# A hybrid encoder layer with 32 experts on one core: the token lists' entries, the buffers of gathered rows and the place of a visit's first transposes are changed

## The chip, the cores and the metric

The kernel runs on one core of a Trainium2 chip, as one launch. The metric is the device time of a launch in microseconds; smaller is better.

## What is computed

One layer over x of 1024 tokens by 1024 features, float32. First comes the mixer: a modulated norm, one projection, windowed attention with a sink and neighbourhood attention side by side, an output projection and a gated residual. Then comes a mixture of 32 experts of which each token takes four, and a final norm. The reference for the second part, cut:

```python
def moe_ffn(h, w_router, b_router, w_gate_up, b_gate_up, w_down, b_down):
    logits = (xt @ w_router + b_router).astype(jnp.float32)
    top_val, top_idx = lax.top_k(logits, TOP_K)          # 4 of 32
    gates = jax.nn.softmax(top_val, axis=-1)
    ...
    def expert_block(args):
        xb, e = args
        gu = xb @ w_gate_up[e] + b_gate_up[e]
        gate = jnp.minimum(gu[:, :D_FF], SWIGLU_LIMIT)
        up = jnp.clip(gu[:, D_FF:], -SWIGLU_LIMIT, SWIGLU_LIMIT)
        glu = gate * jax.nn.sigmoid(SWIGLU_ALPHA * gate)
        return ((up + 1.0) * glu) @ w_down[e] + b_down[e]
    ...
    y = jax.ops.segment_sum(ys * slot_gate[:, None].astype(ys.dtype), slot_tok, num_segments=t + 1)[:t]
```

## The kernel before

**Precision.** Large products are made of three: each float32 operand is split into a rounded part (`hi`) and the remainder (`lo`), and hi·hi, hi·lo and lo·hi are added up in PSUM.

**Output projection and routing.** Until about 560 us the mixer is computed. Then the eight token tiles of 128 go through a pipeline of stages, each some steps behind the one before: `mix` (first 512 columns of the output projection, through `half`), `mix_on` (the other 512, then the norm of the experts' input, stored to `d_h`), `turn_h` (transposes), `logits`, `top`, `places`, `gates_y`, `first_y`. `half` multiplies the projection by the gate and adds it to x: L1016 evicts the PSUM tile `pab`, L1017 and L1018 are the product and the sum, on POOL for the first half of a tile and on DVE for the second. `places` makes four list entries per token: `pi` (L1092) is the position in the experts' list, `pair` (L1094, L1095) holds the row number and the gate. POOL scatters them to the lists `d_l` in HBM (L1097, an indirect DMA per choice), and `first_y` uses `pair` once more as the rows of a scatter-add into `d_y` (L1126). `pi` has two buffers and `pair` has three, so a tile's entries can be written only when the DMAs of an earlier tile have read theirs.

**The first expert, early.** After four tiles `lead` picks the fullest expert so far, starts the load of its first weights (L1181), reads 256 entries of its list (L1160) and gathers their rows into two `xg` tiles (L1164). `xform` transposes them on PE (L1366) and splits them into `xH` and `xL` (L243 on ACT, L244 on DVE). Its products are put between those of the last tiles' routing.

**The visits.** `rank` sorts the experts by load, and `experts` makes a visit to each: wide visits (stream H: several row blocks, weights stationary or moving, L1532 to L1534 and L1557) and narrow ones (stream L, at most 128 rows, L236 to L238). A visit is cut into pieces, (visit, gate/up or down, column, k half), and the pieces of the two streams are merged into one list. For piece m, `load` issues the weights on SP (1 MB each, L1181 or L1184), `cook` makes their hi part on ACT (L1305) and their lo part on DVE and POOL (L1307), and `mm` issues the products. Cooking runs five pieces ahead of the products (`LOOK`). Raw and cooked weights lie in ten slots, of which the first 32 pieces use two for their loads. Before a visit, `get_lists` reads its lists (L1317, SP), `get_rows` gathers its rows into an `xg` tile (L1347, POOL), one of two buffers, and `xform` transposes them. `leave` adds the result to `d_y` (L1490, POOL). At piece 12 (`BEGUN`) the first narrow visit is prepared: lists, gather, transposes, bias. Every later visit is prepared while its stream's previous visit runs: its first gather stands one step before the last gate/up piece, then each down piece issues the next gather and the transposes of the current block.

The order of each engine's instructions is set by a scheduler that works on the order in which the code is written and on the buffers.

Of the kernel before, what the change touches and what calls it, by code (L numbers as in the profile page):

```python
# [5 lines left out]
F32 = mybir.dt.float32  # L6
F32R = mybir.dt.float32r
I32 = mybir.dt.int32
U32 = mybir.dt.uint32
AF = mybir.ActivationFunctionType  # L10
ALU = mybir.AluOpType
# [4 lines left out]
D = 1024  # L16
S = 1024
NT = 8
# [13 lines left out]
NP = 8 // KP  # L32
# [194 lines left out]
class Kernel:  # L227
# [771 lines left out]
    def half(self, x, m):  # L999
        nc, pq, bc, wo, i = self.nc, self.pq, self.bc, self.wo, x["i"]  # L1000
        V, A, P = nc.vector, nc.scalar, nc.gpsimd
        ts = slice(i * 128, (i + 1) * 128)
        cs = slice(512 * m, 512 * m + 512)
        xt, ya = x["xt"][:, cs], x["ya"][:, cs]
        pp = [self.pm.tile([128, 512], F32, name="pab", bufs=4) for _ in range(2)]
        for a in range(2):
            for k in range(4 * a, 4 * a + 4):
                last = self.mm3(pp[a], self.oh[:, k, ts], self.ol[:, k, ts], wo[k][0][:, cs], wo[k][1][:, cs],
                         k % 4 == 0, k % 4 == 3)
        if i == m == 0:  # L1010
            with self.tc.issue_after(last):
                self.sum_squares(1, self.sq, pq.tile([128, 512], F32, name="pt", bufs=1)[:, 0:2 * NT])
            A.activation(self.sqr, self.sums, AF.Sqrt, bias=self.eps, scale=1.0 / 512)
            V.reciprocal(self.sqr, self.sqr)
        A.activation(ya, pp[0], AF.Copy, scale=self.sqr[:, 0, i:i + 1])
        V.scalar_tensor_tensor(ya, pp[1], self.sqr[:, 1, i:i + 1], ya, op0=ALU.mult, op1=ALU.add)  # L1016
        (V if m else P).tensor_tensor(ya, ya, bc["gate_m"][:, cs], op=ALU.mult)  # L1017
        (V if m else P).tensor_tensor(xt, xt, ya, op=ALU.add)  # L1018
        A.activation(ya, xt, AF.Square, accum_out=x["ss"][:, m:m + 1])

    def mix_on(self, x, **_):
# [58 lines left out]
    def places(self, x, macc, gd, lo32, ie, ip, **_):  # L1080

        nc, qp, pr, w, oh, mk, i = self.nc, self.qp, x["pr"], x["w"], x["oh"], x["mk"], x["i"]
        V, P, T = nc.vector, nc.gpsimd, nc.tensor
        ixf, gt = w[:, 0, :], w[:, 1, :]
        T.matmul(pr[:, 192:224], lo32, mk, start=True, stop=False)
        T.matmul(pr[:, 192:224], self.ones, macc, start=False, stop=True)
        V.tensor_tensor(macc, macc, mk, op=ALU.add)
        rk = qp.tile([128, 4, 32], F32, name="rk", bufs=2)
        V.tensor_tensor(rk, oh, pr[:, None, 192:224].to_broadcast([128, 4, 32]), op=ALU.mult)
        V.tensor_reduce(w[:, 4, :], rk, axis=AX.X, op=ALU.add)  # L1090
        pi = qp.tile([128, 4], I32, name="pi", bufs=2)
        V.scalar_tensor_tensor(pi, ixf, float(PITCH), w[:, 4, :], op0=ALU.mult, op1=ALU.add)  # L1092
        pair = x["pair"] = qp.tile([128, 4, 2], I32, name="pair", bufs=3)
        V.tensor_scalar(pair[:, :, 0], ip.to_broadcast([128, 4]), float(PITCH + 128 * i), None, op0=ALU.add)  # L1094
        V.tensor_copy(pair.bitcast(F32)[:, :, 1], gt)  # L1095
        for j in range(4):
            s = P.indirect_dma_start(out=self.d_l, out_offset=bass.IndirectOffsetOnAxis(ap=pi[:, j:j + 1], axis=0),  # L1097
                                     in_=pair[:, j, :], in_offset=None)
            for o in self.scat:
                self.tc.declare_no_dep(s.ins, o.ins, reason="other rows of the lists")  # L1100
            self.scat.append(s)
        V.tensor_tensor(rk, oh, gt[:, :, None].to_broadcast([128, 4, 32]), op=ALU.mult)
        V.tensor_reduce(gd[:, i, :], rk.rearrange("p j e -> p e j"), axis=AX.X, op=ALU.add)
# [143 lines left out]
    def experts(self):  # L1247
# [10 lines left out]
            for x, y in zip(mine, mine[1:]):  # L1258
                nxt[x] = y
        regs, raw, cooked, lists, blk, biases, late = {}, {}, {}, {}, {}, {}, []  # L1260
        xs, hs, accs, gates = {}, {}, {}, {}
        self.pe_time = 0.0
        led = self.led
        regs[0] = led["reg"]
# [76 lines left out]
        def get_rows(n, j):  # L1341

            st, r, blocks = vis[n]
            off, nt = blocks[j]
            ls = lists[n][j]
            xg = self.ep.tile([128, D], F32, name="xg", bufs=2)
            P.indirect_dma_start(out=xg[:nt], out_offset=None, in_=self.d_h2,  # L1347
                                 in_offset=bass.IndirectOffsetOnAxis(ap=ls[:nt, 0:1], axis=0))
            blk.setdefault(n, []).append(dict(n=n, j=j, nt=nt, ls=ls, xg=xg))
# [57 lines left out]
        def xform(b):  # L1407
            n, j = b["n"], b["j"]
            if j == 0:
                xs[n] = parts("x", n)  # L1410
            turn(b["xg"][:b["nt"]], xs[n][1][j][1:], b["nt"], 0, n == 0)
# [168 lines left out]
        for m in range(-LOOK, M):  # L1580
            if m == BEGUN:
                lp = pools["lp"] = tc.alloc_tile_pool(name="lp", bufs=1, side="right", reuse_waits="tile")
                pw = tc.alloc_tile_pool(name="pw", bufs=1, space=PSUM, reuse_waits="tile")
            for j, i in loads_at.get(m, []):
                load(j, i)
            if m < 0:
                cook(m + LOOK)
                continue
            if m == BEGUN:
                n = first[1]  # L1590
                get_lists(n)
                for j in range(len(vis[n][2])):
                    get_rows(n, j)
                    xform(blk[n][j])
                get_bias(n)
                mates = no_mates()
                for b in blk[n]:
                    b["mates"] = mates
                for n in first:
                    get_lists(nxt[n])  # L1600
            n, kind, c, kh = seq[m]
            if m + LOOK < M:
                cook(m + LOOK)
            mm(m)
            if m < BEGUN:
                yield
            if n in nxt:
                q = nxt[n]
                nb = len(vis[q][2])
                at = todo.setdefault(n, 0)  # L1610
                if kind == "g" and c == 3 and kh == NP - 2:
                    if q in nxt:
                        get_lists(nxt[q])
                    get_rows(q, 0)
                if kind == "d":
                    if at < nb:
                        if at + 1 < nb:
                            get_rows(q, at + 1)
                        xform(blk[q][at])
                    if at == 0:  # L1620
                        get_bias(q)
                    if at == 2 * NP - 1:
                        mates = no_mates()
                        for b in blk[q]:
                            b["mates"] = mates
                    todo[n] = at + 1
# [115 lines left out]
```

## Time and profile before

| | |
|---|---|
| runs | 2266.4, 2270.0, 2276.2 us (median 2270.0) |
| profiled execution | 2269.7 us; span 2268.0 us, mean granted clock 0.969 |
| PE busy | 2084.2 us (92%) |
| DVE, POOL, ACT busy | 1568.2 (69%), 1111.3 (49%), 949.6 us (42%) |
| HBM | 518 MB read, 59 MB written, 254 GB/s over the span |

PE is TensorE, DVE VectorE, ACT ScalarE, POOL GpSimd and SP the engine that issues most DMAs; PEld is TensorE's weight load. Times count from the start of the span. An instruction stands as line, operation and output<-input, and the L numbers are lines of the kernel before. A granted clock of 1.00 is 2.4 GHz, 0.50 is 1.2 GHz. Busy shares are averages over stages with different limits, so the rows below are given by stage.

### The profile page before, as it was taken

What the parts mean: (1) busy time and instruction counts of PE and PEld (TensorE: products, weight loads), DVE (VectorE), ACT (ScalarE), POOL (GpSimd) and SP (SyncE); (2) the same over time, 40 slices, a digit from 0 to 9 for tenths busy, and PEclk for the clock granted to TensorE, in tenths of its full rate; (3) what the DMA queues carried; (4) which work ended last, traced back from release to release, by engine and by line L of the source; (5) the groups of instructions that cost most, each with busy time, mean ns of one, the idle gap of its engine ahead of it and who ended that gap; (6) DMA issues with size and microseconds to landing.
All of it is one profiled execution on the core that took longest, in us unless ns stands there. A gap on an engine that the chain in (4) does not pass through costs nothing. (4 is left out here: it accounts for less than half of the span.)

```text
span 2268.0 us, 34804 instructions
## 1 busy us (share of the span) xinstructions
PE 2084.2 (92%) x12090; PEld 1533.8 (68%) x12090; DVE 1568.2 (69%) x2790; ACT 949.6 (42%) x1612; POOL 1111.3 (49%) x959
## 2 busy tenths in 40 slices
PE   6999999999787998888879999999999999999973
PEld 3987777777576876665546555566686777877772
DVE  3777646876585699787866454455686868878975
ACT  3543436764353456554643121222233434345543
POOL 2522123543555567778874334333536455555453
PEclk8999999999899999999989999999999999999987
DMA  9555577823556699898879998999898898898775
GB/s 320 157 166 149 163 217 198 159 78 124 152 164 191 233 298 307 278 293 256 299 225 368 371 320 292 344 347 329 263 347 265 309 315 307 304 313 298 257 251 188
DMA packets 325114, 579.17 MB, mean 255 GB/s; under 512 B 40009, under 2 KB 78089, under 8 KB 322577
## 3 DMA queue, kind: packets, MB, share of 16 engines
q1 hardware_dynamic: 301529, 524.22, 67.7%
q0 software_dynamic: 23408, 52.71, 11.2%
q8 instruction: 97, 1.59, 0.3%
q14 instruction: 80, 0.66, 0.1%
HBM read 518.23 MB, written 58.92 MB: 254 GB/s over the span
## 5 line engine op out<-in xcount | busy, mean ns | idle before, releaser
L1307 POOL TENSOR_TENSOR w<-w,w 128x288 fp32r<-128x288 f32 x456 | 599.9, 1366 | 547.7 <-ACT w L1305 523.6
L1305 ACT ACTIVATE w<-w 128x1024 fp32r<-128x1024 f32 x456 | 469.1, 1054 | 525.3 <-DMA w<-in_w_gate_up 123.8
L1307 DVE TENSOR_TENSOR w<-w,w 128x736 fp32r<-128x736 f32 x456 | 504.8, 1119 | 214.1 <-ACT w L1305 211.9
L1534 PE MATMUL accH<-xH,w 128*128 128x256 f32 (+9 forms) x1408 | 396.8, 294 | 5.1 <-POOL w L1307 4.1
L1532 PE MATMUL accH<-xH,w 128*128 128x256 f32 (+6 forms) x1024 | 320.6, 316 | 2.2 <-ACT xH L243 0.6
L1533 PE MATMUL accH<-xH,w 128*128 128x256 f32 (+6 forms) x1024 | 315.2, 309 | 0.3 <-DVE xH L244 0.3
L1534 PEld LDWEIGHTS accH<-xH,w 128*128 128x128 f32 x1408 | 267.0, 191 | 18.3 <-POOL w L1307 4.8
L1532 PEld LDWEIGHTS accH<-xH,w 128*128 128x128 f32 x1024 | 193.0, 189 | 50.5 <-issue 27.4
L1533 PEld LDWEIGHTS accH<-xH,w 128*128 128x128 f32 x1024 | 193.7, 189 | 5.1 <-DVE xH L244 0.7
L1557 PE MATMUL accL<-w,xL 128*32 128x512 f32 (+3 forms) x896 | 176.9, 599 | 1.2 <-issue 0.8
L236 PE MATMUL accH<-w,hH 128*128 128x512 f32 (+3 forms) x368 | 150.1, 410 | 5.1 <-ACT w L1305 5.1
L237 PE MATMUL accH<-w,hH 128*128 128x512 f32 (+3 forms) x368 | 146.8, 399 | 0.0
L238 PE MATMUL accH<-w,hH 128*128 128x512 f32 (+3 forms) x368 | 143.2, 401 | 1.0 <-POOL w L1307 1.0
L238 PE MATMUL accL<-w,xL 128*72 128x512 f32 (+4 forms) x256 | 106.5, 416 | 39.9 <-POOL w L1307 28.6
L1530 PE MATMUL accH<-xH,w 128*128 128x416 f32 (+2 forms) x384 | 110.6, 365 | 10.1 <-DVE t L1422 10.0
L1490 POOL DMA_INDIRECT d_y<-y,lsH x54 | 96.6, 1789 | 45.6 <-DVE y L1484 32.9
L236 PE MATMUL accL<-w,xL 128*72 128x512 f32 (+4 forms) x256 | 104.3, 407 | 2.2 <-ACT w L1305 1.1
L1449 DVE TENSOR_TENSOR t<-accL,biasL 32x512 f32<-32x512 f32 (+8 forms) x88 | 60.5, 688 | 64.2 <-PE accL L1557 45.4
L236 PEld LDWEIGHTS accH<-w,hH 128*128 128x128 f32 (+3 forms) x368 | 68.4, 186 | 52.4 <-issue 19.2
L237 PE MATMUL accL<-w,xL 128*72 128x512 f32 (+4 forms) x256 | 103.4, 404 | 0.0
L1557 PEld LDWEIGHTS accL<-w,xL 128*32 128x32 f32 (+3 forms) x896 | 39.5, 115 | 84.6 <-issue 79.0
L237 PE MATMUL pm<-whi,hl 128*128 128x256 f32 x320 | 92.5, 290 | 1.4 <-DVE hl L244 1.2
(362 smaller groups left out, 4422.7 us busy)
## 6 DMA issues: line engine op xcount, KB each, us to landing
w<-in_w_gate_up SPq DMA_DIRECT2D x264, 1024.0 KB
w<-in_w_down SPq DMA_DIRECT2D x132, 1024.0 KB
aw<-in_w_ada SPq DMA_DIRECT2D x64, 256.0 KB
wraw<-in_w_in SPq DMA_DIRECT2D x18, 512.0 KB
xt<-in_x SPq DMA_DIRECT2D x16, 512.0 KB
wa<-in_w_ada SPq DMA_DIRECT2D x8, 1024.0 KB
d_h<-zero SPq DMA_DIRECT2D x9, 512.0 KB
d_y<-zero SPq DMA_DIRECT2D x18, 256.0 KB
```

What stands on the lines that cost most here:

```text
L236: mm(ps, lh, rh, start=start, stop=False)
L237: mm(ps, ll, rh, start=False, stop=False)
L238: return mm(ps, lh, rl, start=False, stop=stop).ins
L1305: A.activation(hi, w, AF.Copy)
L1307: eng.tensor_tensor(lo[:, :, cs], w[:, :, cs], hi[:, :, cs].bitcast(F32), op=ALU.subtract)
L1449: V.tensor_tensor(t, p[o:o + nt], bv[o:o + nt], op=ALU.add)
L1490: s = P.indirect_dma_start(out=self.d_y[c], out_offset=bass.IndirectOffsetOnAxis(ap=b["ls"][:nt, 0:1], axis=0), in_=y, in_offset=None, com ...
L1530: mm(p[:, :2 * sp], hi[:, k, ws], x[:, :, kk, :], start=kk == 0, stop=False)
L1532: mm(p[:, :sp], hi[:, k, ws], x[:, 0, kk, :], start=kk == 0, stop=False)
L1533: mm(p[:, :sp], hi[:, k, ws], x[:, 1, kk, :], start=False, stop=False)
L1534: mm(p[:, :sp], lo[:, k, ws], x[:, 0, kk, :], start=False, stop=kk == 7)
L1557: mm(p[o:o + nt], w[:, kk, :], hi[:, k, :], start=kk < len(at), stop=kk >= 8 - len(at))
```

## The change

Five edits. The products L1017 and L1018 of the last tile's first half move from POOL to DVE. `pi` and `pair` get a buffer for each of the eight tiles. Every third gather uses a tile `xg3` of its own. The first narrow visit's transposes are written three pieces after its gather. Of a later visit with several blocks the second gather is written with the last gate/up piece, and in the down pieces a block's transposes stand before the gather of the block after next.

```diff
@@ half
-        (V if m else P).tensor_tensor(ya, ya, bc["gate_m"][:, cs], op=ALU.mult)
-        (V if m else P).tensor_tensor(xt, xt, ya, op=ALU.add)
+        e = V if m or i == NT - 1 else P
+        e.tensor_tensor(ya, ya, bc["gate_m"][:, cs], op=ALU.mult)
+        e.tensor_tensor(xt, xt, ya, op=ALU.add)
@@ places
-        pi = qp.tile([128, 4], I32, name="pi", bufs=2)
+        pi = qp.tile([128, 4], I32, name="pi", bufs=NT)
...
-        pair = x["pair"] = qp.tile([128, 4, 2], I32, name="pair", bufs=3)
+        pair = x["pair"] = qp.tile([128, 4, 2], I32, name="pair", bufs=NT)
@@ experts: get_rows
-            xg = self.ep.tile([128, D], F32, name="xg", bufs=2)
+            got.append(n)
+            xg = (self.ep.tile([128, D], F32, name="xg", bufs=2) if len(got) % 3 else
+                  wp.tile([128, D], F32, name="xg3"))
@@ experts: the loop over pieces
             if m == BEGUN:
                 n = first[1]
                 get_lists(n)
-                for j in range(len(vis[n][2])):
-                    get_rows(n, j)
-                    xform(blk[n][j])
+                get_rows(n, 0)
+                blk[n][0]["mates"] = no_mates()
                 get_bias(n)
-                mates = no_mates()
-                for b in blk[n]:
-                    b["mates"] = mates
                 for n in first:
                     get_lists(nxt[n])
+            if m == BEGUN + 3:
+                xform(blk[first[1]][0])
...
+                if kind == "g" and c == 3 and kh == NP - 1 and nb > 1:
+                    get_rows(q, 1)
                 if kind == "d":
                     if at < nb:
-                        if at + 1 < nb:
-                            get_rows(q, at + 1)
                         xform(blk[q][at])
+                        if at + 2 < nb:
+                            get_rows(q, at + 2)
```

In the order rows below the changed kernel's lines are two to four higher (L1092 is L1094, L1094 is L1096, L1305 is L1307, L1347 is L1351, L1366 is L1370).

DVE, at the last tile's output projection, before. `ip` is the token number within a tile, `rk` and `gd` belong to the gates, `lg` are the next tile's logits.

```order
L1092 SCALAR_TENSOR_TENSOR pi<-w 128x4
L1102 TENSOR_TENSOR rk<-ohot,w 128x128
L1103 TENSOR_REDUCE gd<-rk 128x32
L1094 TENSOR_SCALAR pair<-ip 128x4
L1016 SCALAR_TENSOR_TENSOR ya<-pab,sqr,ya 128x512
L1062 COPY lg<-pr 128x32
```

The same place in the changed kernel:

```order
L1094 SCALAR_TENSOR_TENSOR pi<-w 128x4
L1104 TENSOR_TENSOR rk<-ohot,w 128x128
L1105 TENSOR_REDUCE gd<-rk 128x32
L1016 SCALAR_TENSOR_TENSOR ya<-pab,sqr,ya 128x512
L1064 COPY lg<-pr 128x32
L1019 TENSOR_TENSOR ya<-ya,gate_m 128x512
```

The write of the row numbers is gone from here. All eight (`L1096 TENSOR_SCALAR pair<-ip 128x4 x8`) now stand together ahead of the routing. The eviction L1016 of the last half tile follows the gates directly, and the product and sum of the first half (L1019, L1020) stand some rows earlier on DVE.

ACT, when the first narrow visit's rows have been transposed, before. `hH` is the first expert's activation, `xL<-pt` the narrow visit's split, `w_...` are pieces of weights copied:

```order
L243 ACTIVATE hH<-ga 128x256 x4
L243 ACTIVATE xL<-pt 128x512 x2
L1305 ACTIVATE w_7514<-w_7287 128x1024
L1305 ACTIVATE w_7548<-w_7408 128x1024
L1305 ACTIVATE w_7625<-w_7546 128x1024
```

And now:

```order
L243 ACTIVATE hH<-ga 128x256 x4
L1307 ACTIVATE w_7499<-w_7287 128x1024
L1307 ACTIVATE w_7533<-w_7408 128x1024
L243 ACTIVATE xL<-pt 128x512 x2
L1307 ACTIVATE w_7625<-w_7531 128x1024
```

The two splits moved behind two copies, those of the next two down pieces.

ACT a little later, up to the start of the second wide visit, before; `xH<-pt` are the splits of that visit's row blocks:

```order
L243 ACTIVATE xH<-pt 128x4x128 x2
L1305 ACTIVATE w_7778<-w_7715 128x1024
L1305 ACTIVATE w_7800<-w_7715 128x1024
L1305 ACTIVATE w_7820<-w_7776 128x1024
L1305 ACTIVATE w_7836<-w_7776 128x1024
L243 ACTIVATE xH<-pt 128x4x128
L1305 ACTIVATE w_7858<-w_7818 128x1024
L1305 ACTIVATE w_7880<-w_7818 128x1024
L243 ACTIVATE xH<-pt 128x4x128
L243 ACTIVATE xH<-pt 128x8x56
L1305 ACTIVATE w_7914<-w_7852 128x1024
```

And now:

```order
L243 ACTIVATE xH<-pt 128x4x128 x2
L1307 ACTIVATE w_7719<-w_7608 128x1024
L1307 ACTIVATE w_7749<-w_7608 128x1024
L1307 ACTIVATE w_7778<-w_7717 128x1024
L1307 ACTIVATE w_7800<-w_7717 128x1024
L243 ACTIVATE xH<-pt 128x4x128 x2
L1307 ACTIVATE w_7820<-w_7776 128x1024
L1307 ACTIVATE w_7836<-w_7776 128x1024
L243 ACTIVATE xH<-pt 128x8x56
L1307 ACTIVATE w_7858<-w_7818 128x1024
```

The third block's two splits, which stood behind w_7836 and behind w_7880, stand now together ahead of w_7820; the last block's (8x56) moved ahead of w_7858 and w_7880.

On PE the narrow visit's eight transposes (L1366, now L1370) have not moved: they stand behind the ranking's two small products and ahead of the first product of the next down piece in both. On POOL the wide visit's third gather (56 rows of lsH) moved ahead of two subtractions (L1307) and two scatter-adds (L1490), and the next narrow visit's gather (120 rows of lsL) ahead of six subtractions, a scatter-add and a clear. L1017 and L1018 of the last tile no longer stand there between the first expert's gathers and the next scatters.

## Rows read from the trace of the kernel before

**Rows 1.** Windows by stage: length; busy PE, PEld, DVE, ACT, POOL; clock; DMA share; GB/s
```profile
567.00:612.00 45.00, 39.64 (x187) 30.60 (x187) 29.32 (x84) 14.68 (x30) 22.90 (x18) 0.92 0.45 124
612.00:634.50 22.50, 9.49 (x47) 7.07 (x46) 9.73 (x23) 9.97 (x19) 11.97 (x12) 0.70 0.62 172
634.50:700.00 65.50, 59.59 (x456) 55.44 (x455) 56.97 (x137) 29.44 (x49) 42.57 (x37) 1.00 0.65 175
700.00:740.00 40.00, 26.31 (x118) 20.98 (x118) 20.41 (x35) 15.59 (x19) 21.09 (x17) 0.85 0.65 197
1190.00:2150.00 960.00, 951.38 (x5430) 651.50 (x5429) 643.35 (x1030) 319.33 (x476) 429.79 (x335) 1.00 0.92 315
```

**Rows 2.** Waits, 567 to 640 us: waiter, releaser, total us, times, longest us
```profile
DVE pair L1094 <- DMA d_l<-pair,pi: 18.3, 2, 12.7
DVE pair L1094 <- DMA d_y<-yi,pair: 7.1, 2, 3.9
```

**Rows 3.** DVE's timeline: start, length, instruction, idle time before it and releaser
```profile
567.33 0.17 DVE L1094 TENSOR_SCALAR pair<-ip 128x4 int32<-128x4 f32 x1 [3.91 <-DMA d_y<-yi,pair]
580.14 0.17 DVE L1094 TENSOR_SCALAR pair<-ip 128x4 int32<-128x4 f32 x1 [5.59 <-DMA d_l<-pair,pi]
627.20 0.17 DVE L1094 TENSOR_SCALAR pair<-ip 128x4 int32<-128x4 f32 x1 [12.68 <-DMA d_l<-pair,pi]
627.30 0.75 DVE L1016 SCALAR_TENSOR_TENSOR ya<-pab,sqr,ya 128x512 f32<-128x512 f32 x1
```

**Rows 4.** PE's timeline at the first expert's transposes and first product
```profile
615.68 2.82 PE L1366 MATMUL accH<-idt,xg 128*128 128x128 f32 x12 [0.82 <-DMA xg<-d_h,ls]
628.11 1.12 PE L1366 MATMUL accH<-idt,xg 128*128 128x128 f32 x4 [9.61 <-DVE ya L1016]
633.21 0.36 PE L1532 MATMUL accH<-xH,w 128*128 128x256 f32 x1 [0.53 <-DVE xH L244]
```

**Rows 5.** POOL's timeline: the last scatter of tile 3, the gather of its lists
```profile
600.79 1.32 POOL L1097 DMA_INDIRECT d_l<-pair,pi  x1 [0.30 <-issue]
609.56 1.76 POOL L1164 DMA_INDIRECT xg<-d_h,ls  x1 [7.44 <-DMA ls<-d_l]
```

**Rows 6.** PE's timeline at the first narrow visit
```profile
704.29 1.97 PE L1366 MATMUL pt<-idt,xg 128*128 128x128 f32 x8 [4.33 <-DMA xg<-d_h,lsL]
707.89 0.80 PE L236 MATMUL accH<-w,hH 128*128 128x512 f32 x1 [1.63 <-ACT w L1305]
...
738.21 1.07 PE L1366 MATMUL pt<-idt,xg 56*128 56x56 f32 x8 [7.14 <-issue]
739.92 1.41 PE L1532 MATMUL accH<-xH,w 128*128 128x312 f32 x4 [0.63 <-ACT xH L243]
```

**Rows 7.** Windows, the stretch at half clock around the second wide visit's start
```profile
734.70:744.90 10.20, 5.76 (x24) 5.23 (x25) 6.47 (x9) 4.82 (x7) 9.03 (x8) 0.50 0.57 171
```

**Rows 8.** ACT's timeline: copies of the weight pieces that come late
```profile
714.61 2.01 ACT L1305 ACTIVATE w<-w 128x1024 fp32r<-128x1024 f32 x2 [5.83 <-DMA w<-in_w_down]
721.95 2.01 ACT L1305 ACTIVATE w<-w 128x1024 fp32r<-128x1024 f32 x2 [5.33 <-DMA w<-in_w_down]
734.00 2.00 ACT L1305 ACTIVATE w<-w 128x1024 fp32r<-128x1024 f32 x2 [6.89 <-DMA w<-in_w_gate_up]
735.91 0.58 ACT L243 ACTIVATE xH<-pt 128x512 fp32r<-128x512 f32 x1
```

**Rows 9.** SP's timeline: when the loads of two of them went out
```profile
709.48 0.41 SPq L1184 DMA_DIRECT2D w<-in_w_down  x1
713.08 0.40 SPq L1184 DMA_DIRECT2D w<-in_w_down  x1
```

**Rows 10.** Waits of ACT, 820 to 1190 us
```profile
ACT w L1305 <- DMA w<-in_w_gate_up: 65.8, 34, 6.3
```

**Rows 11.** Waits of PE, 740 to 1190 us
```profile
PE accL L238 <- POOL w L1307: 29.1, 20, 6.8
```

**Rows 12.** Waits of POOL, 700 to 2150 us
```profile
POOL xg L1347 <- PE pt L1366: 20.0, 10, 4.5
```

More of the change, by code (lines that the diff above doesn't have):

```diff
@@ L1260, in experts @@
         regs, raw, cooked, lists, blk, biases, late = {}, {}, {}, {}, {}, {}, []
-        xs, hs, accs, gates = {}, {}, {}, {}
+        xs, hs, accs, gates, got = {}, {}, {}, {}, []
         self.pe_time = 0.0
```

## The prediction

> **What bounds the kernel now.** I read the busy time by stage first [rows 1]. From 1190 to 2150 us PE is busy for 951.4 of 960 us, and nothing in the change makes PE's work there shorter. So I look for stages in which PE idles and which the diff touches. Two stand out. Between 567 and 634.5 us PE idles for 45.00 − 39.64 = 5.4 and 22.50 − 9.49 = 13.0 us, 18.4 us together. Between 700 and 740 us it idles for 13.7 us. From 634.5 to 700 us, between the two, it works for 59.6 of 65.5 us at full clock, so that a start won earlier should survive that stage.
>
> The table of waits says what DVE stands for in the first stage [rows 2]: it waits four times, 18.3 + 7.1 = 25.4 us, before it may write the row numbers into `pair`, because DMAs of an earlier tile (the scatter to the lists, the scatter-add to `d_y`) still read the old buffer. DVE executes in order, so all that is queued behind the write waits as well. The last wait is the dearest, 12.68 us [rows 3]: directly behind it stands the eviction L1016 at 627.30, and PE's last four transposes of the first expert's rows wait 9.61 us for that eviction [rows 4], since it frees a PSUM tile. The first product of the first expert is then at 633.21.
>
> In the second stage PE stops three times [rows 6]: 4.33 us for the first narrow visit's gather, 1.63 us for a copied weight, and 7.14 us before the transposes of the 56-row block, which the profile puts down to nothing it sees. ACT's timeline explains the last one [rows 8]: the split at 735.91, which frees the PSUM tile for them, stands in ACT's queue behind copies of weights that began only at 734.00, after 6.89 us of waiting for a load.
>
> **The change part by part.** *Buffers of pi and pair.* With eight of each, no write of an entry waits for a DMA, and the eight writes of row numbers move to one place ahead of the routing. All four waits go. What PE gets of it is less than 25.4 us. At the most it gets all its idle time of the stage, 18.4 us, and what the clock would give back: 612 to 634.5 us were granted 0.70 of 2.4 GHz on average [rows 1], and PE's 9.49 us there would be 9.49 × 0.70 = 6.6 at full clock, 2.9 less; 21.3 us together. At the least it gets the one wait that PE itself shows, 9.6 us.
>
> Between these I follow the chain. What is late next is the gather of the first expert's rows. Its chain is: last scatter of tile 3 at 600.79, list read back, gather at 609.56 [rows 5], first transposes at 615.68 [rows 4], 14.9 us that no edit shortens. But tile 3's scatter itself stands behind DVE's waits of 3.91 and 5.59 us [rows 3], 9.5 us, of which PE's own idle time of 5.4 us in 567 to 612 us bounds what can come through. I take 5.5 us, so the first transposes start at about 610.2. The fourth quad follows at once: 610.2 + 2.82 + 1.12 = 614.1. In the run before, 633.21 − 628.11 − 1.12 = 4.0 us lie between the end of that quad and the first product, filled by tile 7's transposes and logits; they stay, at full clock perhaps 3. First product at about 617, so **16 us** earlier.
>
> *Products on DVE.* DVE gets two instructions of the size of L1016, 0.75 us [rows 3], so 1.5 us; the 25.4 us that it no longer waits cover them. Without that cover they would cost 1.5 us. POOL loses two from between the first gathers and tile 4's scatters.
>
> *First narrow visit.* PE's transposes haven't moved in PE's order, so the 4.33 us for the gather stay. On ACT the copies of the next two down pieces stand ahead of the narrow visit's splits now: the 1.63 us for a copy go, and the weight buffers that these copies free let the next loads out some microseconds earlier. *Third gather buffer, gathers and transposes in another order.* The wide visit's third block is split ahead of two copies that wait for loads, and its last gather is issued earlier. So the 7.14 us go, and the 0.63 us behind them. At the most this gives 1.63 + 7.14 + 0.63 = 9.4 us and half of the 5.76 us that PE worked at half clock (0.50, 1.2 GHz) from 734.7 to 744.9 us [rows 7], 12.3 us. At the least it gives nothing, if the loads decide. I take **9 us**, near the upper end, because the waits that go are named and their instructions have moved in the order.
>
> *What is given back.* From 820 to 1190 us ACT waits 65.8 us for weights [rows 10]: there the stream of loads leads, and PE keeps a gain only as far as the loads start earlier too. Loads go out as PE frees buffers, so most of the gain travels with them, but the part won at the narrow visit does so only partly. I take **2 us** back, between nothing and the whole 9. The later visits' hoisted gathers I cost at nothing: PE shows no wait for a gather later, and the stage to 2150 us is PE's own.
>
> **Sum.** 16 + 9 − 2 = 23 us. The profiled execution took 2269.7 us (span 2268.0), 0.3 us from the median of the runs. 2269.7 − 23 = 2246.7, so **2247 us**.
>
> **The rivals.** *Only the pair part pays.* Gathers that start earlier run beside the loads of weights that ACT waits for. The trace has it in small: a load issued at 709.48 was copied from 714.61 on, after 5.1 us; the next, issued at 713.08, only at 721.95, after 8.9 us [rows 8, 9], and between them the wide visit's gathers were issued on POOL. If the copies come later by this 3.8 us twice, the 9 us are nearly gone: 2269.7 − 16 = 2254 us. Against it: the loads themselves go out earlier. The Trainium skill, "DMA: Bandwidth & Descriptors", section "Issuing engines are not separate DMA queues", speaks for this rival: DMAs started by different engines run on the same 16 DMA engines and interleave. By that rule the sum would lose its second term and be 2254 us; the two loads above agree with it, though they show the delay once only. I give it 0.24.
>
> *The wait for the gather takes the place.* If tile 3's scatter comes hardly earlier, because POOL's own queue or the DMAs' landing set it, the gather lands as before and only the 9.61 us go; with little left of the second part the time is 2258 to 2260 us. For it: POOL already waits 7.44 us for the list [rows 5]. Against it: the scatter is behind DVE's two waits. 0.13, half of it on the faster side of the bound.
>
> *Slower: gathers block the subtractions.* POOL runs in order, and a gather placed earlier finds its buffer still read by transposes. POOL waited for that 10 times, 20.0 us, at the longest 4.5 [rows 12]. Behind it stand subtractions for which PE already waits 29.1 us between 740 and 1190 us [rows 11]. If ten gathers wait 4.5 us each and PE gets all of it, 45 us come on top: 2247 + 45 = 2292 us. It is slower than before by the bound from 34 us on, 3.4 us a gather. Against it: there is a third buffer now, and most of these gathers lie where PE is full and POOL has time. 0.05.
>
> *The change doesn't do what it says.* The narrow visit's transposes stand where they stood on PE; if ACT and the loads pay nothing either, and the freed DVE only waits elsewhere (its table of waits shows none behind these), the time is 2265 to 2270 us. 0.06.
>
> **How the numbers follow.** About 0.5%, 11.3 us, is what a measurement of this kernel can tell from no change, so faster means below 2258.7 us. The forecast has 0.52: both parts pay, 2236 to 2253 us, from 21.3 + 12.3 = 33.6 us of gain down to 17. Forecast and first rival make 0.76, half of the second 0.06: 0.82 faster. Same: the other half of the second, the last rival: 0.13. Slower: 0.05. The range from 2236 to 2260 us holds the forecast, the first rival and the second.
>
> **What would show it.** Right: no wait of DVE for `pair`; the fourth quad of transposes directly behind the third; the first product of the first expert at about 617 us; no stop of 7 us before the second wide visit, whose first product comes 25 us earlier, near 715 us; from 1190 us on the same work, shifted. Wrong: a new wait of PE for the gather at about 610 us of more than 5 us; copies at the first narrow visit that still wait 5 to 7 us for loads, with PE standing behind them; more than 29 us of PE's waits for POOL's subtractions before 1190 us; or a second wide visit that starts 25 us earlier while the end moves by much less, which would mean that the loads take it back.

## The result, and the profile after

Six runs of the changed kernel had a median of 2247.07 us (2244.74 to 2259.12), those of the kernel before 2271.16 us. The ratio is 0.9903, with a 95% interval of 0.9877 to 0.9928: about 1.0% faster. A second set of six, measured later beside other kernels, gave 2237.15 us and 0.9866 (0.9837 to 0.9896). The forecast was 2247 us. It rests on two terms, though, and the runs below show that the sum came out in part by luck, and for partly other reasons than those given.

The profiled execution of the change took 2252.1 us (span 2250.3), 17.6 us less than that of the kernel before and 5 us above the median of its six.

The view of the tile `pair`, kernel after: each kind of instruction, its count, shortest, median and longest ns, and the start of the first and last in us.

```profile
L1099 POOL DMA_INDIRECT d_l<-pair,pi x32: 954/973/1587, 543.3 to 674.0; - x32
...
L1096 DVE TENSOR_SCALAR pair<-ip x8: 156/157/158, 504.6 to 505.1; 128x4 int32<-128x4 f32 x8
```

and of the kernel before:

```profile
L1097 POOL DMA_INDIRECT d_l<-pair,pi x32: 954/984/1562, 543.1 to 688.3; - x32
```

The eight writes of row numbers now stand together from 504.6 us on, and nothing in this tile's view of after waits, where DVE waited 25.4 us [rows 2]. The last scatter starts 14.3 us earlier (674.0 for 688.3).

PE's timeline after, with what it waited for; these lines answer to [rows 4] and [rows 6]:

```profile
609.47 1.97 PE L1370 MATMUL accH<-idt,xg 128*128 128x128 f32 x8 [4.07 <-DMA xg<-d_h,ls]
611.67 1.94 PE L1370 MATMUL accH<-idt,xg 128*128 128x128 f32 x8 [0.23 <-DMA xg<-d_h,ls]
...
615.78 0.38 PE L1536 MATMUL accH<-xH,w 128*128 128x256 f32 x1
```

```profile
679.94 0.63 PE L1211 MATMUL pr<-rw,ip 32*128 32x32 f32 x2 [5.13 <-DVE rw L1209]
...
693.43 1.09 PE L1370 MATMUL pt<-idt,xg 128*128 128x128 f32 x8 [0.82 <-DMA xg<-d_h,lsL]
...
695.94 0.47 PE L238 MATMUL accH<-w,hH 128*128 128x512 f32 x1 [0.49 <-DVE w L1309]
...
722.40 1.41 PE L1536 MATMUL accH<-xH,w 128*128 128x312 f32 x4 [4.90 <-ACT xH L243]
```

The sixteen transposes of the first expert now run in two groups with a stop of 0.23 us between them; ahead of the last four nothing waits, where it was 9.61 us. What came in its place is a wait of 4.07 us for the gather. The first product (L1536) starts at 615.78, 17.4 us earlier. At the narrow visit the stops of 4.33 and 1.63 us are 0.82 and 0.49 (the first is 3.21 in e10 below), and the stop of 7.14 us ahead of the 56-row block is gone. In its place PE waits 4.90 us for a split at the second wide visit's first product, which starts 17.5 us earlier. And there is a stop that [rows 4, 6] don't show, 5.13 us for the ranking on DVE (L1209), at 679.94; before, the same stop was 1.10 us.

So the gain is 17.4 us at the first product, only 10.9 at the narrow visit's transposes (704.29 to 693.43), 17.5 at the second wide visit and 17.6 at the end.

**One zero mark for all runs.** Executions of one kernel don't reach the routing at the same time: the first scatter of list entries started at 543.1 us before, 543.3 after, and at 538.1 in the second profile of the change (e10), though at most eight small writes ahead of it differ. So I count from that scatter. The table has, for each kernel, the first expert's first product, the narrow visit's first transposes, the second wide visit's first product and the end of the span, in us from the first scatter, and then the lengths between them.

| kernel | first product | narrow transposes | second wide visit | end | lengths |
|---|---|---|---|---|---|
| before | 90.1 | 161.2 | 196.8 | 1724.9 | 71.1, 35.6, 1528.1 |
| after | 72.5 | 150.1 | 179.1 | 1707.0 | 77.6, 29.0, 1527.9 |
| e10, after again | 71.6 | 146.3 | 173.6 | 1696.4 | 74.7, 27.3, 1522.8 |
| e1, buffers | 71.8 | 149.1 | 181.2 | 1710.5 | 77.3, 32.1, 1529.3 |
| e2, all but buffers | 86.3 | 158.9 | 185.9 | 1713.3 | 72.6, 27.0, 1527.4 |
| e3, gathers | 90.4 | 161.6 | 196.9 | 1724.3 | 71.2, 35.3, 1527.4 |
| e4, narrow visit | 90.4 | 160.6 | 188.3 | 1712.4 | 70.2, 27.7, 1524.1 |
| e5, products | 87.9 | 161.0 | 193.5 | 1723.6 | 73.1, 32.5, 1530.1 |
| e6, buffers, products | 70.0 | 147.1 | 181.0 | 1710.6 | 77.1, 34.0, 1529.6 |
| e7, buffers, narrow visit | 71.3 | 150.2 | 178.0 | 1702.2 | 78.9, 27.8, 1524.2 |
| e11, all but narrow visit | 70.0 | 148.2 | 182.0 | 1709.9 | 78.2, 33.8, 1527.9 |

### The profile page after: what moved, and what is told of

The parts are those of the page before. It is cut to its first block, busy times and chain, and to the rows that moved or that the text cites. A ratio compares the mean times of both kernels' runs of the same rounds, so it can differ in the third digit from the quotient of the medians.

```text
span 2250.3 us, 34808 instructions
## 1 busy us (share of the span) xinstructions
PE 2080.6 (92%) x12090; PEld 1534.5 (68%) x12090; DVE 1573.4 (70%) x2792; ACT 950.0 (42%) x1612; POOL 1113.2 (49%) x957
## 5 line engine op out<-in xcount | busy, mean ns | idle before, releaser
L1307 ACT ACTIVATE w<-w 128x1024 fp32r<-128x1024 f32 x456 | 469.1, 1054 | 527.5 <-DMA w<-in_w_gate_up 156.2
L1536 PE MATMUL accH<-xH,w 128*128 128x256 f32 (+6 forms) x1024 | 322.5, 318 | 6.5 <-ACT xH L243 4.9
L1536 PEld LDWEIGHTS accH<-xH,w 128*128 128x128 f32 x1024 | 194.5, 191 | 56.8 <-issue 30.6
L1534 PE MATMUL accH<-xH,w 128*128 128x416 f32 (+2 forms) x384 | 111.5, 367 | 12.1 <-DVE t L1426 12.1
L1561 PEld LDWEIGHTS accL<-w,xL 128*32 128x32 f32 (+3 forms) x896 | 39.4, 115 | 84.4 <-issue 77.3
```

The source lines that it names most:

```text
L1307: A.activation(hi, w, AF.Copy)
L1534: mm(p[:, :2 * sp], hi[:, k, ws], x[:, :, kk, :], start=kk == 0, stop=False)
L1536: mm(p[:, :sp], hi[:, k, ws], x[:, 0, kk, :], start=kk == 0, stop=False)
L1561: mm(p[o:o + nt], w[:, kk, :], hi[:, k, :], start=kk < len(at), stop=kk >= 8 - len(at))
```

## The experiments

Four were sent beside each other first; they take the change apart. Ratios are to the kernel before, from runs on the same chip.

**e1_pair**, the buffers alone:

```diff
-        pi = qp.tile([128, 4], I32, name="pi", bufs=2)
+        pi = qp.tile([128, 4], I32, name="pi", bufs=NT)
-        pair = x["pair"] = qp.tile([128, 4, 2], I32, name="pair", bufs=3)
+        pair = x["pair"] = qp.tile([128, 4, 2], I32, name="pair", bufs=NT)
```

> Only the eight buffers of pi and pair, everything else as before. Theory A (the forecast's split: the buffers give 16 us, the edits at the visits 7): about 2254 us, DVE without a wait for pair, the first product of the first expert near 617 us, the second wide visit 16 us earlier. Theory B (the buffers pay for all, the edits at the visits for nothing): 2247 us, as the whole change. Theory C (the products on DVE are needed for the gain too, because POOL holds up the scatters): less than half, 2260 us or more.

Measured: 2256.11 us, 0.9944 (0.9927 to 0.9961). About half of the gain, as theory A has it in kind, but 12.7 us in place of 16. The first product comes 18.3 us earlier from the zero mark (90.1 to 71.8), more than forecast, and then the stage up to the narrow visit lasts 77.3 us in place of 71.1. The windows of that stage, before and in this kernel (length; PE, PEld, DVE, ACT and POOL busy; clock; DMA share; GB/s):

```profile
633.20:704.30 71.10, 60.88 (x465) 56.42 (x465) 60.01 (x152) 30.74 (x51) 42.79 (x37) 1.00 0.65 178
```

```profile
615.20:692.50 77.30, 65.18 (x464) 60.75 (x464) 62.87 (x151) 32.16 (x53) 47.87 (x41) 0.93 0.64 171
```

As many matmuls (465 and 464) are busy for 60.88 and 65.18 us: the granted clock was 1.00 of 2.4 GHz there before and is 0.93 now. That is 4.3 of the 6.2 us; 1.9 us are more idle time (10.2 to 12.1). The waits show where a part of both comes from (waiter, releaser, total us, times, longest). DVE before and in this kernel, then PE and ACT in this kernel:

```profile
DVE w L1307 <- ACT w L1305: 3.4, 5, 1.1
```

```profile
DVE w L1307 <- ACT w L1305: 9.2, 6, 3.4
```

```profile
PE pr L1124 <- DVE rk L1089: 4.2, 1, 4.2
```

```profile
ACT w L1305 <- DMA w<-in_w_gate_up: 17.2, 4, 5.5
```

DVE now stands for 9.2 us in place of 3.4 ahead of subtractions whose copies ACT has not made, because their weights have not landed (ACT's 17.2 us were 12.5 before). What is queued behind on DVE is the routing: DVE's longest wait, 3.4 us, ends at 626.18, and PE stands for 4.2 us in front of a product of the routing (L1124, at 631.86), a wait that the stage didn't have. After it the granted clock was 0.62 and 0.53 in the windows from 632 to 634 and to 636 us. That is only a part of the lower clock. It was 0.65 and 0.50 from 666 to 670 us and 0.57 and 0.58 from 680 to 684 too, behind stops of 2.08 and 1.77 us for the routing and the ranking. Before, these two stops were 2.04 and 1.10 us, and the clock stayed at 1.00; no run shows why.

Before, PE's long stop lay ahead of the first product, and the loads used it to get ahead. SP's timeline has the first expert's second load, before and in this kernel:

```profile
615.87 0.40 SPq L1181 DMA_DIRECT2D w<-in_w_gate_up  x1
```

```profile
608.55 0.40 SPq L1181 DMA_DIRECT2D w<-in_w_gate_up  x1
```

It went out 17.3 us ahead of the first product (633.21), and goes out 6.7 us ahead of it now (615.20). No run sends these loads out earlier, so this is read from the traces and not tested.

**e2_no_pair**, the whole change with `pi` at two buffers and `pair` at three:

```diff
-        pi = qp.tile([128, 4], I32, name="pi", bufs=NT)
+        pi = qp.tile([128, 4], I32, name="pi", bufs=2)
-        pair = x["pair"] = qp.tile([128, 4, 2], I32, name="pair", bufs=NT)
+        pair = x["pair"] = qp.tile([128, 4, 2], I32, name="pair", bufs=3)
```

> The whole change without the eight buffers: products on DVE, third gather buffer, later transposes, other order of gathers. Theory A: 7 us of gain, about 2263 us; DVE waits 25 us for pair as before, and the second wide visit starts 7 to 9 us earlier. Theory B: 2270 us, no change; the second wide visit starts as before, because loads of weights or a split behind them hold it.

Measured: 2256.11 us, 0.9941 (0.9924 to 0.9958). The other edits pay 0.59%, about twice what theory A gave them. Its profile starts the routing late (first scatter at 549.3) and took 2264.4 us; from the zero mark the second wide visit comes 10.9 us earlier (196.8 to 185.9).

**e3_rows**, the third gather buffer and the other order of gathers and transposes alone:

```diff
-            xg = self.ep.tile([128, D], F32, name="xg", bufs=2)
+            got.append(n)
+            xg = (self.ep.tile([128, D], F32, name="xg", bufs=2) if len(got) % 3 else
+                  wp.tile([128, D], F32, name="xg3"))
...
+                if kind == "g" and c == 3 and kh == NP - 1 and nb > 1:
+                    get_rows(q, 1)
...
-                        if at + 1 < nb:
-                            get_rows(q, at + 1)
                         xform(blk[q][at])
+                        if at + 2 < nb:
+                            get_rows(q, at + 2)
```

> Only the third gather buffer and the other order of gathers and transposes of the later visits. Theory A: the stop of 7.1 us before the 56-row block goes, 2263 to 2266 us. Theory B: 2270 us; the stop goes from the transposes to the second wide visit's first product.

Measured: 2269.78 us, 0.9992 (0.9974 to 1.001): no change, theory B. PE's and ACT's timelines of this kernel ahead of the second wide visit:

```profile
741.04 1.41 PE L1534 MATMUL accH<-xH,w 128*128 128x312 f32 x4 [6.75 <-ACT xH L243]
```

```profile
735.24 2.00 ACT L1305 ACTIVATE w<-w 128x1024 fp32r<-128x1024 f32 x2 [4.42 <-DMA w<-in_w_gate_up]
737.15 0.58 ACT L243 ACTIVATE xH<-pt 128x512 fp32r<-128x512 f32 x1
738.55 2.00 ACT L1305 ACTIVATE w<-w 128x1024 fp32r<-128x1024 f32 x2 [0.83 <-DMA w<-in_w_gate_up]
740.46 0.52 ACT L243 ACTIVATE xH<-pt 128x448 fp32r<-128x448 f32 x1
```

The stop of 7.14 us ahead of the 56-row block did go, and came back whole as one of 6.75 us at the first product, for the last split at 740.46. That split still stands behind two copies (738.55) whose weights have just landed. Here, moving instructions around a load that comes late only moved the wait.

**e4_narrow**, only the first narrow visit's transposes written three pieces behind its gather:

```diff
-                for j in range(len(vis[n][2])):
-                    get_rows(n, j)
-                    xform(blk[n][j])
+                get_rows(n, 0)
...
+            if m == BEGUN + 3:
+                xform(blk[first[1]][0])
```

> Only the first narrow visit's transposes written three pieces after its gather. Theory A: the 1.6 us for a copied weight go, and little more: 2266 to 2269 us. Theory B: 2270 us.

Measured: 2259.63 us, 0.9961 (0.9946 to 0.9976): 8.8 us, where I had given this edit 1.6 and some earlier loads. The stretch from the narrow transposes to the second wide visit is 27.7 us in place of 35.6. ACT's timeline there, before:

```profile
698.66 0.42 ACT L243 ACTIVATE hH<-ga 128x256 fp32r<-128x256 f32 x1 [0.35 <-DVE ga L1434]
705.44 0.60 ACT L243 ACTIVATE xL<-pt 128x512 fp32r<-128x512 f32 x1 [6.37 <-PE pt L1366]
706.30 0.60 ACT L243 ACTIVATE xL<-pt 128x512 fp32r<-128x512 f32 x1 [0.26 <-PE pt L1366]
706.79 1.99 ACT L1305 ACTIVATE w<-w 128x1024 fp32r<-128x1024 f32 x2
```

ACT's and SP's timelines of this kernel:

```profile
697.03 0.42 ACT L243 ACTIVATE hH<-ga 128x256 fp32r<-128x256 f32 x1 [0.35 <-DVE ga L1434]
697.35 1.04 ACT L1305 ACTIVATE w<-w 128x1024 fp32r<-128x1024 f32 x1
699.93 1.06 ACT L1305 ACTIVATE w<-w 128x1024 fp32r<-128x1024 f32 x1 [1.54 <-issue]
702.82 0.60 ACT L243 ACTIVATE xL<-pt 128x512 fp32r<-128x512 f32 x1 [1.84 <-PE pt L1366]
```

```profile
701.68 0.41 SPq L1184 DMA_DIRECT2D w<-in_w_down  x1
```

The copies of the next two down pieces start at 697.35 and 699.93, right behind the first expert's last split. Before, they stood behind the narrow visit's splits, the splits behind its transposes, and those behind the gather that landed at 704.29 [rows 6]. The next load waits for DVE's subtraction behind these copies (SP's table of waits has 12.5 us for it before, 7.3 here). So the load that went out at 709.48 [rows 9] goes out at 701.68, 7.8 us earlier (5.7 from the zero mark), and the stream behind it.

The same 118 matmuls lie in the stretch. Of the 7.9 us that it is shorter, 1.5 are PE's busy time (26.23 and 24.77 us, at a granted clock of 0.84 and 0.93); the rest are the stops behind the gather, 7.1, 1.6 and 0.6 us before and one of 2.9 now. PE's wait for the gather itself is still there, 3.34 us for 4.33. So the wait that cost was not that one; it was that weight copies stood in the same queue behind it.

A second set of four asked whether these add up.

**e5_prod**, only the last tile's two products on DVE:

```diff
-        (V if m else P).tensor_tensor(ya, ya, bc["gate_m"][:, cs], op=ALU.mult)
-        (V if m else P).tensor_tensor(xt, xt, ya, op=ALU.add)
+        e = V if m or i == NT - 1 else P
+        e.tensor_tensor(ya, ya, bc["gate_m"][:, cs], op=ALU.mult)
+        e.tensor_tensor(xt, xt, ya, op=ALU.add)
```

> Only the last tile's two products on DVE. Theory A (DVE stands in a wait of 12.7 us right behind, which covers them; POOL's scatters of tile 4 start 2.6 us earlier and end the wait earlier): 2266 to 2268 us. Theory B (they only move): 2267 to 2268 us, as before; on DVE 1.4 us more.

Measured: 2264.39 us, 0.997 (0.9949 to 0.999), some 7 us less and below what either theory had. Its first product comes 2.1 us earlier from the zero mark. The profiled execution shows 1.3 us at the end, so the size is open.

**e6_pair_prod**, the diff of e1_pair and that of e5_prod together.

> The eight buffers of pi and pair with the two products on DVE, nothing at the visits. The buffers alone took 0.56% off. Theory A (the effects add up, and the products are worth nothing): the same, 2254 to 2256 us. Theory C (with the buffers the products on POOL stand in the way of the scatters): 3 us or more below the buffers alone, 2252 us or less.

Measured: 2254.53 us, 0.9934 (0.9908 to 0.9959), the same as the buffers alone within the intervals. The first product comes 1.8 us earlier than with the buffers alone (70.0 for 71.8), and the end is the same (1710.6 and 1710.5): theory A, theory C falls.

**e7_pair_narrow**, the diff of e1_pair and that of e4_narrow together.

> The eight buffers of pi and pair with the narrow visit's later transposes, without the products, the third gather buffer and the other order of gathers. Alone the first took 0.56% off and the second 0.39%. Theory A (they work at different places and add up): 0.95%, about 2246 us, as the whole change. Theory D (both end at the same thing, the stream of weight loads before the second wide visit): about 2254 us, no more than the buffers alone.

Measured: 2245.32 us, 0.9886 (0.9859 to 0.9913). Theory A: the two add up (0.56% and 0.39% alone), and these two edits give what the whole change gives. Products, third buffer and the other order of gathers need not be there, as far as these intervals tell.

**e9_after_k5**, the whole change, five pieces in place of three:

```diff
-            if m == BEGUN + 3:
+            if m == BEGUN + 5:
                 xform(blk[first[1]][0])
```

> The whole change with the narrow visit's transposes written five pieces behind the gather in place of three. On ACT six copies now stand ahead of the first of its two splits in place of two, and on PE the transposes stand behind down pieces. Theory E (the gain at the narrow visit comes from copies that don't wait behind the splits, and PE's wait for the gather goes too): 1 to 4 us below the whole change, 2243 to 2246 us. Theory F (two copies are enough, the loads decide from there): the same as the whole change, 2245 to 2248 us, or later if the narrow visit's products wait for the splits.

Measured: 2240.74 us, 0.9858 (0.9828 to 0.9888). Against the first set of the whole change this looked like theory E, against the second (0.9866) like theory F. From the zero mark the second wide visit starts where it does in the profile of after (178.7 and 179.1; 173.6 in e10). So no gain of five pieces over three is shown; that two copies are enough fits this, within intervals of 0.3% either way.

The last set ran the whole change again as its measure.

**e10_after**, the changed kernel itself, with no edit.

> The changed kernel once more, as the measure for the other runs of this row: 0.99 of the kernel before, 2245 to 2249 us. Its second profile shows whether the stop of 5.1 us before the ranking belongs to the kernel or to that one execution: theory G (to the kernel) 4 us or more again; theory H (to the execution) 3 us or less, with the second wide visit 2 to 3 us earlier.

Measured: 2237.15 us, 0.9866 (0.9837 to 0.9896), below the 2245 to 2249 that I expected. Theory H: PE's stops in this profile, ranking, gather of the narrow visit, second wide visit:

```profile
671.40 0.40 PE L1211 MATMUL pr<-rw,ip 32*128 32x32 f32 x2 [1.25 <-DVE rw L1209]
...
684.41 1.59 PE L1370 MATMUL pt<-idt,xg 128*128 128x128 f32 x8 [3.21 <-DMA xg<-d_h,lsL]
...
711.68 1.04 PE L1536 MATMUL accH<-xH,w 128*128 128x312 f32 x4 [2.35 <-ACT xH L243]
```

The ranking is waited for 1.25 us, not 5.13, and the second wide visit starts 173.6 us from the zero mark in place of 179.1. The stop of 5 us belonged to that one execution, in which the copy that DVE waited for came late: ACT waited 5.54 us for its weights there and 1.62 in e10. The ranking stands behind that subtraction in DVE's order in both.

**e11_no_narrow**, the whole change with the narrow visit's transposes back at its gather:

```diff
-                get_rows(n, 0)
...
+                for j in range(len(vis[n][2])):
+                    get_rows(n, j)
+                    xform(blk[n][j])
...
-            if m == BEGUN + 3:
-                xform(blk[first[1]][0])
```

> The whole change without the narrow visit's later transposes: buffers, products, third gather buffer and order of gathers stay. The narrow edit alone took 0.39% off the kernel before. Theory A (it is what pays at the visits): 8 to 10 us more than the whole change, about 2255 us, as the buffers alone, and the first load behind the narrow visit's splits goes out 7 to 8 us later relative to the first expert's last split. Theory I (with the third gather buffer it isn't needed): as the whole change, 2246 us.

Measured: 2253.47 us, 0.9931 (0.991 to 0.9951), 16 us more than the whole change beside it; theory A, and more than its 8 to 10. ACT and SP here:

```profile
687.58 0.42 ACT L243 ACTIVATE hH<-ga 128x256 fp32r<-128x256 f32 x1 [0.34 <-DVE ga L1438]
691.65 1.08 ACT L243 ACTIVATE xL<-pt 128x512 fp32r<-128x512 f32 x2 [3.65 <-PE pt L1370]
692.62 2.00 ACT L1307 ACTIVATE w<-w 128x1024 fp32r<-128x1024 f32 x2
```

```profile
695.32 0.41 SPq L1186 DMA_DIRECT2D w<-in_w_down  x1
```

From the first expert's last split (687.58) to the load it is 7.7 us; in e10 the same load went out at 684.56, 4.7 us behind the split at 679.90. That is 3.0 us, not the 7 to 8 expected: with the buffers the gather lands sooner behind the first expert's end (the transposes start 3.4 us behind the last split here, 5.6 in the kernel before). The stretch from the narrow transposes to the second wide visit is 33.8 us in place of 27.3. The rest of the 16 us, in the stages before and behind it, is no larger than what two profiles of the whole change differ by (10.6 us at the end), so the edit's size here stays rough. The third gather buffer doesn't replace it.

**e12_two20** and **e13_k5_two20** tried to go on from there: only loads of the first 20 pieces are held to two raw slots, the others may take any free one; e13 has the five pieces of e9 besides.

```diff
 ALONE = 32
+TWO = 20
...
-            if m < ALONE:
+            if m < TWO:
                 ok = first[0] <= a
...
-        if m < ALONE:
+        if m < TWO:
             first = sorted([first[1], end + 1])
...
-        if what == "load" and m < ALONE:
+        if what == "load" and m < TWO:
             able = [0, 1]
```

> The whole change, with the weight loads limited to two raw slots for the first 20 pieces in place of 32, so that the loads around the first narrow visit go out earlier. Theory J (the stretch from the narrow visit to the second wide visit hangs on loads that wait for a raw slot): the wait of PE for the second wide visit's split goes, and the time is 4 to 8 us below the whole change, about 2240 us. Theory K (the loads are given back later, where PE waits for weights anyway): as the whole change, 2245 to 2248 us.

> As the run before, with the narrow visit's transposes five pieces behind the gather. Alone five in place of three stood at 0.986 of the kernel before. Theory J: the sum of both, 2236 us. Theory K: 2240 us, as with five pieces alone.

Measured: 2257.19 us, 0.9945 (0.9926 to 0.9964), and 2259.5 us, 0.9962 (0.9945 to 0.998). Both theories miss: they are slower than the whole change by some 20 us. SP, ACT and PE in e12:

```profile
665.90 1.53 SPq L1187 DMA_DIRECT2D w<-in_w_down  x3
679.60 0.34 SPq L1320 DMA_DIRECT2D lsL<-d_l  x1
693.10 0.35 SPq L1341 DMA_DIRECT2D biasL<-in_b_gate_up  x1
...
697.28 0.41 SPq L1184 DMA_DIRECT2D w<-in_w_gate_up  x1
```

```profile
684.09 3.89 ACT L1308 ACTIVATE w<-w 128x1024 fp32r<-128x1024 f32 x4
706.36 2.01 ACT L1308 ACTIVATE w<-w 128x1024 fp32r<-128x1024 f32 x2 [18.38 <-DMA w<-in_w_gate_up]
```

```profile
699.13 0.79 PE L239 MATMUL accH<-w,hH 128*128 128x512 f32 x1 [6.04 <-POOL w L1310]
...
716.84 1.97 PE L1371 MATMUL pt<-idt,xg 128*128 128x128 f32 x8 [4.67 <-DVE xL L245]
```

Three down loads went out within 1.5 us from 665.90 on, two of them some 30 us earlier than in after (695.91 and 699.51), and ACT made four copies in a row at 684.09. But the next load went out at 697.28, and ACT then waited 18.38 us for it: SP issued nothing between the list at 679.60 and the bias at 693.10, and the lists of the wide visit and the load stood behind. PE's wait for the second wide visit's split did go, as theory J has it, and others came: 6.04 us for a subtraction on POOL and 4.67 for a split. Why the bias load stood 13 us wasn't tried. SP's table of waits puts 12.9 us of it to the last part of DVE's ranking (L1243, at 692.78; 13.0 us in e13), for which DVE in turn stood 3.17 and 3.56 us behind small products on PE. In after the bias load goes out at 682.74, ahead of that part of the ranking, and SP has no such wait. So here the loads hung on the ranking; whether the earlier down loads brought that about, no run tests.

## Why the prediction was right, point by point

**Sum and range.** 23 us were forecast, 1.0%; measured were 0.97% and, the second time, 1.34%. Both medians lie in the range. That the sum fits so well is in part luck. Its first term was too large (16 us; 12.7 to the end by e1), its second, of which the cause was wrong, near or too small (9 us; 8.8 by e4, 13.4 by e2, which has the products too), and the 2 us given back did not show. The second wide visit was to start 25 us earlier; from the zero mark it is 17.7 us in after and 23.2 in e10.

**Buffers of pi and pair, 16 us.** The mechanism is as described up to the first product: all four waits are gone, the fourth quad follows the third, the gather is late next (4.07 us in after, 2.13 in e10, below the 5 us that would have spoken against it). At the first product it is even 17.6 us from the zero mark in after and 18.5 in e10. The step that failed is the sentence that a start won earlier should survive the stage up to 700 us because PE is busy there: the stage got longer in all six profiles of the table that have the buffers, 74.7 to 78.9 us in place of 71.1, at a granted clock of 0.91 to 0.95 in place of 1.00. PE busy for 59.6 of 65.5 us said that PE was full while its weights had a head start, not that it would be full without one: in these six the second load leads the first product by 6.6 to 11.2 us, not 17.3. To the end the buffers are worth 0.56%, 12.7 us (e1).

**Products, nothing.** Within the intervals with the buffers (e6 and e1); alone, where DVE's waits for `pair` are still there, they took 0.3% off (e5). So the forecast that they cost 1.5 us without cover isn't borne out either.

**Visits, 9 us, and 2 back.** The size was near, the cause wrong. I put 7.14 + 0.63 us on the third gather buffer and the order of gathers, because the named waits' instructions had moved. e3 has these moved instructions and no gain. The step that failed is that an instruction which moves takes its wait along: [rows 8] have the 6.89 us that the copies wait for a load, and that load came no sooner. The gain is that of the later transposes, 0.39% alone (e4) and 0.65% as the difference between e11 and e10, for which I had priced the 1.63 us and left "the next loads out some microseconds earlier" without a price. That was the term: a load that goes out 5.7 us earlier from the zero mark, and a stretch to the second wide visit that is 7.9 us shorter. The 7.14 us do go in e4, because the loads come earlier. The prediction had loads go out as PE frees buffers; here SP waited for DVE's subtractions. The rows to see it were there: the splits of the narrow visit stand ahead of two copies in ACT's order, and both behind a gather that lands at 704.29.

**Given back, 2 us.** Not seen. From the second wide visit to the end it is 1528.1 us before, 1527.9 in after, 1522.8 in e10 and 1524.1 in e4. Among the kernels with the later transposes, e4, e7, e9 and e10 have 1520.7 to 1524.2 us there, but e2, after, e12 and e13 1527.4 to 1530.0, as all those with the transposes at the gather have (1527.4 to 1530.1). So in some of these profiles 3 to 7 us more are gained behind the second wide visit's start; where they come from wasn't followed.

**Rivals.** That only the pair part pays (2254 us) is refuted by e2 and e4. The delay that it rests on is there before and after: a load that went out at 699.51 in after was copied from 707.65 on, 8.1 us later, as 8.9 before [rows 8, 9]. By the Trainium skill, "DMA: Bandwidth & Descriptors", section "Issuing engines are not separate DMA queues", DMAs of different engines interleave on the same 16 DMA engines; both delays agree with this, but no run here shows that the gathers cause them or that they take anything from the gain. That the gather lands as before is refuted too: the first transposes start at 609.47 in place of 615.68, 6.2 us earlier, near the 610.2 that were forecast. That gathers block the subtractions isn't seen either: over the 450 us from the second wide visit PE waits 24.2 us for POOL's subtractions in after and 23.0 in e10, 29.1 before [rows 11]. That the change doesn't do what it says holds for three of its five edits: the third buffer and the other order of gathers are together worth nothing that the runs can tell (e3), and neither are the products beside the buffers (e6).

## What to carry to other kernels

When an instruction waits long, ask first what is queued behind it on the same engine and who starts a transfer from there: here copies of weights behind a split that waited for a gather cost 8 us, while the wait that PE itself showed for that gather hardly changed (4.33 and 3.34 us). A wait ahead of a stage that hangs on a stream of loads can hide that the loads are late; before counting on its removal, see whether the next stage has its weights without that head start. And a stop that goes when instructions are reordered must be looked for at the next instruction that needs the same late transfer before it is counted as gain.

## What the runs showed that was not expected

Executions of one kernel on one core differ already before the changed part: the first list scatter started anywhere from 538.1 to 549.3 us in the profiles of this study, in kernels that differ ahead of it by eight small writes at most. This spread of 11 us is as large as an edit's effect. Counted from that scatter, some profiles agree closely: the ends of e1, e6 and e11, whose medians lie within 3 us, lie within 0.7 us of each other, 14.2 to 14.9 us ahead of the kernel before. But the two profiles of the whole change still differ by 10.6 us at the end, as their two medians do by 9.9.
